# Memory values head by head in 256 columns, and the feed-forward's activation sums moved: at once in layer 0, over four products in layer 1

## The chip, the core and the metric

The kernel runs on one NeuronCore of a Trainium2 chip. Its engines are TensorE (PE: matmuls, and PEld: its weight loads), VectorE (DVE), ScalarE (ACT), GpSimd (POOL, which here only issues DMAs that accumulate) and SyncE (SP, which issues the other DMAs). The metric is the device time of one execution in microseconds, as a median of several runs.

## The reference, cut to what matters

Two decoder layers over x (512 tokens of 1024), with 256 memory tokens:

```python
z = rmsnorm(h, g_mix[i]) @ w_in[i]
# layer 0: causal pooling over 2, 4, 8, 16 tokens; layer 1: differential attention, 4 heads
mem_out = memory_attention(z_memq, mem, g_mem[i], w_mem_kv[i])    # 4 heads of 256
h = h + jnp.concatenate([mix, mem_out], axis=-1) @ w_out[i]
h = h + swiglu(rmsnorm(h, g_ffn[i]), w_gate[i], w_up[i], w_down[i])    # 2816 hidden
```

All is float32. The memory's values are the second half of `rmsnorm(mem) @ w_mem_kv[i]`: 256 tokens by 4 heads of 256 columns.

## The kernel before, in words

**Numbers as two halves.** Every float32 operand is split into a rounded part `hi` (an ACT copy, line 174 or 177) and the rest `lo` (a DVE subtraction, line 175 or 178); a product is three matmuls, hi·hi, hi·lo and lo·hi (`three`). So each 512 KB weight tile costs one ACT and one DVE instruction of 1024 columns ahead of its 12 or 24 matmuls. `weights()` loads and splits two tiles ahead (`AHEAD`); there are three buffers each for the raw tile and its halves (`N_W`).

**The order.** PE's instructions stay in the order in which the code is written; `Pace` writes it by interleaving generators on a rough clock, in which "rest" and "need" hold a task back. The other engines' orders come from the tile framework's scheduler; each engine then runs its queue in order. `FIRST` (layer 0) and `SECOND` (layer 1) list the units of the stage ahead of the output projection: `q`, `k`, `v` are the queries, keys and values of memory heads, `i` and `o` the pooling's input and output products, `Q`, `K`, `V` those of the differential attention, `h`, `a`, `b` tiles of the output projection. A star makes a unit wait until the previous head's scores are done. Beside it runs `mem_chain`: for each head scores (`msc`), softmax, transposes (`mtr`), split (`mpth`, `mptl`), and the product with the values (`mo`).

**Memory values.** `mem_values(l, b)` makes two heads at once: stationary the memory tokens, moving 512 columns of weights, 48 matmuls in four weight tiles, and two PSUM banks. `token_major`, used for the differential values `V`, makes one head from two weight tiles with 256 moving columns.

**Feed-forward.** `ffn_up` works on blocks of 512 hidden columns and replaces eight quarter products by seven (numbered 1 to 7, run in the order 1, 2, 5, 3, 6, 7, 4; 24 matmuls each). Products 5, 6, 3, 7 need sums of activations: `Norm7.__call__` splits `h[k]` as each output tile of the projection is finished, and in the first block (u = 0) `later` makes the sums: `sums124` during product 1 (for q = 0 to 3: `xs`, `xt`, `xc`, `xe`) and `sum3` during product 2 (`xd`, `xa`). Products 1 and 6, 7, 4 use PSUM tiles `ffr`, product 2 `ffz`, products 5 and 3 `ffq`. After product 5 its result is copied out (`c`, line 721) before product 3 goes on in the same bank. The SiLU (line 738) waits for the norm's factor `rcf`, which a chain of small DVE instructions makes from transposed sums of squares (`ps_st`, lines 281 to 316).

Of the kernel before, what the change touches and what calls it, by code (L numbers as in the profile page):

```python
# [8 lines left out]
F32 = mybir.dt.float32  # L9
# [3 lines left out]
AF = mybir.ActivationFunctionType  # L13
ALU = mybir.AluOpType
AX = mybir.AxisListType

P = 128
D = 1024
S = 512
NM = 256  # L20
DFF = 2816
KD = D // P
# [9 lines left out]
G_MIX, G_FFN, G_MEM, G_KV, G_FINAL, G_POOL, G_SUB = 0, 16, 32, 48, 56, 64, 72  # L32
# [4 lines left out]
AHEAD = 2  # L37
AHEAD7 = 2
EARLY7 = 2
R_H = 3.3  # L40
R_SM = 6.6
R_T = 1.98
R_DP = 4.4
# [11 lines left out]
R_N1 = 1.0  # L55
OUT = ((0, 1), (2, 3), (4, 5), (6,), (7,))
R_C = 4.5
SECOND = "Q0 k0 q0 k1 v0 q1* Q1 k2 q2* Q2 k3 v1 Q3 q3* K0 h0 h1 h2 V0 h3 h4 K1 V1 h5 K2 V2 K3 a0 a1 a2 V3 a3 h6 h7 b0 b2 b1 b3"
WARM = (256, 256, 256, 256)
FIRST = "q0 q1 k0 i0 i2 i1 o0 k1* v0 o1 i3 o2 k2 v1 q2* o3 k3 q3*"  # L60
PARTS = 2
START = "x0 p0 x1 x2 x3 p1 x4 x5 s0 r0 x6 x7 s1 w3 r1 s2 s3 r2 r3 s4 s5 s6 s7"

# [39 lines left out]
def trunk(ctx, tc, xT, memT, w_in, w_out, w_out1, w_gate, w_up, w_down, w_mk, w_mv, pool_w, w_k, w_v,  # L103
          gains, lams, c_ident, c_mask, c_rope, c_cnt, out):
    nc = tc.nc
# [14 lines left out]
    def slot(name, shape=(2, S), dtype=F32R, parts=P):  # L120

        return slots.tile([parts, *shape], dtype, tag="s", name=name)
# [7 lines left out]
    def duo(name):  # L130

        t = slot(name)
        return t[:, 0, :], t[:, 1, :]

    def tt(name="t"):
        return tmp.tile([P, S], F32, tag="t", name=name)

    def mmps(name="mm"):
        return ps_mm.tile([P, S], F32, tag="mm", name=name)
# [31 lines left out]
    def split(src, hi, lo, scale=None):  # L171

        if scale is None:
            queued(A.copy(out=hi, in_=src))  # L174
            queued(V.tensor_tensor(out=lo, in0=src, in1=f(hi), op=ALU.subtract))  # L175
        else:
            queued(A.activation(out=hi, in_=src, func=AF.Copy, scale=scale))
            queued(V.scalar_tensor_tensor(out=lo, in0=src, scalar=scale, in1=f(hi), op0=ALU.mult, op1=ALU.subtract))


    class Load:
# [4 lines left out]
        def __init__(self, src, kt, cols):  # L186
            self.src, self.kt, self.cols = src, kt, cols
# [4 lines left out]

        def part(self, ks):
            raw, hi, lo = [t[:, ks, :] for t in (self.raw, self.hi, self.lo)]
            if len(self.src.shape) == 3:
                nc.sync.dma_start(out=raw, in_=self.src[:, ks, :])
            else:

                raw, hi, lo = raw.rearrange("p n (k c) -> p n k c", k=2), *[t.rearrange("p k (n c) -> p n k c", n=2) for t in (hi, lo)]
                nc.sync.dma_start(out=raw, in_=self.src)  # L200
            split(raw, hi, lo)

        def fetch(self):
# [17 lines left out]
    def weights():  # L221

        used[0] += 1
        load_to(used[0] + (AHEAD if isinstance(plan[min(used[0], len(plan) - 1)], Load) else AHEAD7))
        return loaded[used[0] - 1]

    def unit(loads, go, need=None):
        plan.extend(x if hasattr(x, "parts") else Load(*x) for x in loads)
        return go, need
# [11 lines left out]
    def gain(base, k):  # L241
        return g_sb[:, base + k:base + k + 1]
# [87 lines left out]
    class Norm7:  # L330
# [1 line left out]

        def __init__(self, base, minus):
            self.base, self.minus, self.sums = base, minus, Sums()
            self.of, self.xa = {n: [None] * 4 for n in (1, 2, 3, 4, 5, 6, 7)}, [None] * 4

        def __call__(self, k):
            q, of = k % 4, self.of  # L340
            if k < 4:
                a, b = self.xa[q] = duo("xa")
                split(h[k][:, :NM], a[:, :NM], b[:, :NM], gain(self.base, k))
                of[1][q] = a[:, :NM], b[:, :NM]
            else:
                a, b = duo("xb")
                split(h[k], a, b, gain(self.base, k))
                of[2][q], of[4][q] = (a[:, :NM], b[:, :NM]), (a[:, NM:], b[:, NM:])
            self.sums.add(h[k])

        def sums124(self, q):
            g, gq, mq = gain(self.base, q + 4), gain(self.base, q), self.minus[:, q:q + 1]
            one, two = slice(0, NM), slice(NM, S)
            x, t = tt("xs"), tt("xt")
            A.activation(out=x, in_=h[q + 4], func=AF.Copy, scale=g)
            V.scalar_tensor_tensor(out=t[:, one], in0=h[q][:, two], scalar=gq, in1=x[:, two], op0=ALU.mult, op1=ALU.subtract)
            V.scalar_tensor_tensor(out=t[:, two], in0=h[q][:, one], scalar=mq, in1=t[:, one], op0=ALU.mult, op1=ALU.add)
            a, b = duo("xc")
            split(t, a, b)
            self.of[5][q], self.of[6][q] = (a[:, one], b[:, one]), (a[:, two], b[:, two])  # L360
            V.tensor_tensor(out=x[:, one], in0=x[:, one], in1=t[:, two], op=ALU.add)
            if q % 2 == 0:
                self.last = duo("xe")
            a, b = [x_[:, (q % 2) * NM:(q % 2 + 1) * NM] for x_ in self.last]
            split(x[:, one], a, b)
            self.of[3][q] = a, b

        def sum3(self, q):
# [5 lines left out]

        def later(self, product, i):

            for q in (2 * i, 2 * i + 1):
                if product == 1:
                    self.sums124(q)
                elif product == 2:  # L380
                    self.sum3(q)

    def x_split(base, k, xs):
        a, b = duo("x")
# [86 lines left out]

        return unit([(src[c], 4, 256) for c in range(2)], go)

    def mem_values(l, b):


        def go():
            pss = [mmps("v") for _ in range(2)]
            x = mem_x[l]
            for i in range(KD // 2):  # L480
                whi, wlo = weights()
                for k in range(2):
                    xh, xl = x[0][2 * i + k], x[1][2 * i + k]
                    for t, ps in enumerate(pss):
                        tk = slice(t * P, (t + 1) * P)
                        yield from group(ps, three(xh[:, tk], xl[:, tk], whi[:, k, :], wlo[:, k, :]),
                                         i == 0 and k == 0, i == KD // 2 - 1 and k == 1)
            yield "spawn", leave(pss)

        def leave(pss):  # L490
            yield "need", "m_row"
            heads = [duo("v") for _ in range(2)]
            for t, ps in enumerate(pss):
                for n, (a, b_) in enumerate(heads):
                    i, o = slice(n * 256, (n + 1) * 256), slice(t * 256, (t + 1) * 256)
                    split(ps[:, i], a[:, o], b_[:, o], m_col[:, t:t + 1])
            for n, v in enumerate(heads):
                mem_v[l, 2 * b + n] = [v]
                pace.at(("mv", l, 2 * b + n), 5.0)

        return unit([(w_mv[l, 2 * b:2 * b + 2, i // 2, :, 2 * (i % 2):2 * (i % 2) + 2, :].rearrange("n p k c -> p n k c"), 2, 2 * 256)
                     for i in range(KD // 2)], go)


    def mem_queries(l, n, xs, need=None, at_once=False):
# [167 lines left out]
    def ffn_up(l, norm, rc, hid):  # L673
        def one(u):
# [6 lines left out]
            def product(p, pss, start=False):  # L681
                more = {} if start else {"skip_group_check": True}

                def part(i, t, whi, wlo):
                    tk = slice(t * P, (t + 1) * P)
                    terms = []
                    for k in range(2):
                        xh, xl = norm.of[p][2 * i + k]
                        terms += [(xh[:, tk], whi[:, k, :]), (xl[:, tk], whi[:, k, :]), (xh[:, tk], wlo[:, k, :])]
                    yield from group(pss[t][:, :w], terms, start and i == 0, i == 1, **more)  # L690

                if p in (5, 7):

                    ws = [weights() for _ in range(2)]
                    for t in range(2):
                        for i in range(2):
                            yield from part(i, t, *ws[i])
                    return
                for i in range(2):
                    ws = weights()  # L700
                    if u == 0:
                        norm.later(p, i)
                    for t in range(2):
                        yield from part(i, t, *ws)
# [286 lines left out]
    norm0, norm1, xk = Norm(G_MIX), Norm(G_MIX + 8), ([], [])  # L991
    minus = const.tile([P, 2 * KD], F32, name="minus")
    V.tensor_scalar_mul(minus, g_sb[:, G_FFN:G_FFN + 2 * KD], -1.0)
    norm_f = [Norm7(G_FFN, minus[:, :KD]), Norm7(G_FFN + 8, minus[:, KD:])]
    rcf = [const.tile([P, NT], F32, name=f"rcf{l}") for l in range(2)]
    hid = [], []
    hids = [([], []), ([], [])]
# [259 lines left out]
```

## Time and profile before

| | us |
|---|---|
| median of 3 runs | 1378.43 (1378.07 to 1380.15) |
| the profiled execution, its own time | 1381.14 |
| its span, first to last instruction | 1379.4 |
| PE busy in the span | 1344.4 (97%) |
| DVE busy | 839.9 (61%) |
| ACT busy | 666.7 (48%) |

The span is cut below into stretches in which one can count the matmuls that have to run, at the rate that undisturbed stretches show; what a stretch takes beyond that is lost. PE's busy time alone doesn't show the loss, since a matmul at a lower clock is also busy.

### The profile page before, as it was taken

To read this page: it belongs to the slowest core of one execution; us is meant where nothing else is said; L and a number is where in the kernel's file an instruction comes from. 1 tells how busy PE (TensorE), PEld (TensorE's weight loads), DVE (VectorE), ACT (ScalarE), POOL (GpSimd) and SP (SyncE) were. 2 spreads that over 40 slices of the span, in tenths; PEclk is the share of its full clock that TensorE was granted. 3 is DMA by queue.
4 is the path that set the end of the run, shared out by engine and by line. 5 is a ranking of instruction groups with operands and counts; after the bars stand their busy time and mean duration, and the time that the engine had idled before them with its cause. 6 is when DMAs were issued, how large, how long until landed. Compare 5 with 4: busy or idle time off the path is not lost.

```text
span 1379.4 us, 17573 instructions
## 1 busy us (share of the span) xinstructions
PE 1344.4 (97%) x6746; PEld 1132.1 (82%) x6746; DVE 839.9 (61%) x1366; ACT 666.7 (48%) x1093; POOL 103.2 (7%) x84
## 2 busy tenths in 40 slices
PE   9998999989999999999999899999999999999997
PEld 7887888868888888888888788888877888888886
DVE  8877543575566584336556655678596655576323
ACT  7444432455555573324545534455375555556421
POOL 0000000022222200000000000000012222200000
PEclk9999999989999999999999999999999999999999
DMA  6343323588889913334423222221269899843331
GB/s 233 108 138 84 123 77 92 135 157 164 186 183 166 200 41 98 101 98 147 136 84 120 87 61 77 77 77 62 86 146 186 171 205 160 160 108 96 100 96 61
DMA packets 111156, 168.57 MB, mean 122 GB/s; under 512 B 5920, under 2 KB 84512, under 8 KB 111072
## 3 DMA queue, kind: packets, MB, share of 16 engines
q1 hardware_dynamic: 67856, 124.67, 28.7%
q0 software_dynamic: 42240, 41.95, 20.0%
q8 instruction: 53, 0.87, 0.3%
q10 hardware_dynamic: 976, 0.82, 0.2%
q14 instruction: 31, 0.25, 0.1%
HBM read 165.33 MB, written 2.10 MB: 121 GB/s over the span
## 4 chain that ended last, share of the span: by engine, by line
PE 71%; DVE 4%; ACT 2%; issue 1%; DMA 1%; POOL 0%; DVEq 0%; ACTq 0%; POOLq 0%
PE down L151 17%; PE ffr L151 16%; PE qk L151 6%; PE ffq L151 6%; PE wo L151 6%; PE v L151 5%; PE ffz L151 4%; PE mq L151 3%; PE mk L151 2%; PE htr L154 1%; DVE wlo L175 1%; PE dsc L151 1%; PE do L151 1%; ACT whi L174 1%; PE msc L151 1%; PE mo L151 1%
## 5 line engine op out<-in xcount | busy, mean ns | idle before, releaser
L175 DVE TENSOR_TENSOR wlo<-raw,whi 128x1024 fp32r<-128x1024 f32 (+2 forms) x226 | 267.7, 1186 | 257.1 <-ACT whi L174 256.5
L174 ACT CAST whi<-raw 128x1024 fp32r<-128x1024 f32 (+2 forms) x226 | 230.9, 1022 | 392.5 <-PE down L151 120.3
L151 PE MATMUL down<-hidp,whi 128*128 128x512 f32 (+1 forms) x748 | 220.4, 378 | 1.8 <-ACT hidp L174 1.1
L175 DVE TENSOR_TENSOR wlo<-rawa,whi 128x1024 fp32r<-128x1024 f32 (+1 forms) x108 | 117.3, 1086 | 85.5 <-ACT whi L174 81.8
L151 PEld LDWEIGHTS down<-hidp,whi 128*128 128x128 f32 x748 | 137.5, 188 | 28.3 <-ACT hidp L174 1.6
L174 ACT CAST whi<-rawa 128x1024 fp32r<-128x1024 f32 (+1 forms) x108 | 101.6, 941 | 104.9 <-PE ffr L151 58.7
L151 PE MATMUL down<-hidp,wlo 128*128 128x512 f32 (+1 forms) x374 | 140.9, 377 | 0.0
L646 POOL DMA_DIRECT2D rawa<-in_w_up x40 | 51.5, 1287 | 1038.7 <-DVE wlo L175 1007.4
L151 PE MATMUL ffr<-whi,xa 128*128 128x512 f32 (+1 forms) x384 | 112.1, 376 | 0.0
L151 PEld LDWEIGHTS down<-hidp,wlo 128*128 128x128 f32 x374 | 70.4, 188 | 12.9
L151 PE MATMUL mq<-x,whi 128*128 128x512 f32 x256 | 80.0, 393 | 0.8 <-ACT whi L174 0.6
L151 PE MATMUL qk<-x,whi 128*128 128x512 f32 x256 | 80.7, 397 | 0.0
L151 PE MATMUL wo<-mo,whi 128*128 128x512 f32 x256 | 79.4, 392 | 0.0
L151 PEld LDWEIGHTS ffr<-whi,xa 128*128 128x128 f32 x384 | 68.7, 189 | 11.8 <-ACT c L726 0.4
L151 PE MATMUL ffr<-wlo,xa 128*128 128x512 f32 (+1 forms) x192 | 71.5, 372 | 0.0
L151 PE MATMUL ffq<-whi,xe 128*128 128x512 f32 (+1 forms) x192 | 57.8, 385 | 3.7 <-ACT c L721 3.1
L151 PEld LDWEIGHTS mq<-x,whi 128*128 128x128 f32 x256 | 47.8, 189 | 11.7 <-ACT whi L174 1.6
L151 PE MATMUL ffq<-whi,xc 128*128 128x512 f32 (+1 forms) x192 | 57.2, 383 | 0.0
L151 PE MATMUL ffr<-whi,xb 128*128 128x512 f32 (+1 forms) x192 | 55.7, 374 | 0.4 <-DVE c L731 0.4
L151 PE MATMUL ffz<-whi,xb 128*128 128x512 f32 (+1 forms) x192 | 55.6, 373 | 0.0
L151 PEld LDWEIGHTS qk<-x,whi 128*128 128x128 f32 x256 | 47.8, 190 | 9.4
L151 PEld LDWEIGHTS wo<-mo,whi 128*128 128x128 f32 x256 | 47.4, 188 | 9.4
(234 smaller groups left out, 2712.2 us busy)
## 6 DMA issues: line engine op xcount, KB each, us to landing
rawa<-in_w_up POOLq DMA_DIRECT2D x40, 512.0 KB, 6.0
raw<-in_w_down SPq DMA_DIRECT2D x34, 512.0 KB, 3.6
raw<-in_w_out SPq DMA_DIRECT2D x32, 512.0 KB, 3.5
raw<-in_w_in SPq DMA_DIRECT2D x30, 512.0 KB, 3.8
raw<-in_w_gate SPq DMA_DIRECT2D x20, 512.0 KB, 4.8
rawa<-in_w_gate SPq DMA_DIRECT2D x20, 512.0 KB, 5.8
raw<-in_w_up SPq DMA_DIRECT2D x20, 512.0 KB, 5.0
raw<-in_w_up POOLq DMA_DIRECT2D x20, 512.0 KB, 6.1
```

The source lines that it names most:

```text
L151: tc.keep_in_program_order(nc.tensor.matmul(ps, lhsT=l, rhs=r, start=start, stop=stop, **more))
L154: tc.keep_in_program_order(nc.tensor.transpose(out=out, in_=in_, identity=ident))
L174: queued(A.copy(out=hi, in_=src))
L175: queued(V.tensor_tensor(out=lo, in0=src, in1=f(hi), op=ALU.subtract))
L646: nc.gpsimd.dma_start(out=t, in_=src, accum_op=ALU.add)
```

## The change

Five edits.

1. `mem_values` becomes a call of `token_major` for one head: 48 matmuls with 256 moving columns and two weight tiles a head. The special form in `Load.part` goes.
2. `FIRST` and `SECOND` list the four heads' values apart and in other places. In layer 0: v0, then `o1`, v1, then `i3`; v2 before `q3`, v3 last. In layer 1: v0, then `q1`, v1; v2 and v3 between `q3` and `K0`.
3. `sums124` is cut into `sum1`, `sum2`, `sum4`; `xc` is split in two halves of 256 columns, and its source `xt` lies in a slot for two q's. In layer 0 (`at_once`) all four sums of a q are made when `h[q + 4]` is finished, within the output projection.
4. In layer 1 they are made in the first block during four products: `sum1` in 1, `sum4` in 2, `sum2` in 5, `sum3` in 3.
5. `R_H`, the rest ahead of the hidden transposes, is 3.7 instead of 3.3.

```diff
-R_H = 3.3
+R_H = 3.7
...
-SECOND = "Q0 k0 q0 k1 v0 q1* Q1 k2 q2* Q2 k3 v1 Q3 q3* K0 h0 h1 h2 V0 h3 h4 K1 V1 h5 K2 V2 K3 a0 a1 a2 V3 a3 h6 h7 b0 b2 b1 b3"
+SECOND = "Q0 k0 q0 k1 v0 q1* v1 Q1 k2 q2* Q2 k3 Q3 q3* v2 v3 K0 h0 h1 h2 V0 h3 h4 K1 V1 h5 K2 V2 K3 a0 a1 a2 V3 a3 h6 h7 b0 b2 b1 b3"
-FIRST = "q0 q1 k0 i0 i2 i1 o0 k1* v0 o1 i3 o2 k2 v1 q2* o3 k3 q3*"
+FIRST = "q0 q1 k0 i0 i2 i1 o0 k1* v0 o1 v1 i3 o2 k2 q2* o3 k3 v2 q3* v3"
...
+            if self.at_once and k >= 4:
+                for part in (self.sum1, self.sum2, self.sum4, self.sum3):
+                    part(q)
+
+        def sum1(self, q):
+
+            x, one, two = tt("xs")[:, :NM], slice(0, NM), slice(NM, S)
+            A.activation(out=x, in_=h[q + 4][:, two], func=AF.Copy, scale=gain(self.base, q + 4))
+            if q % 2 == 0:
+                self.pair = slot("xt", (2, S), F32)
+            t = self.raw[q] = self.pair[:, q % 2, :]
+            V.scalar_tensor_tensor(out=t[:, one], in0=h[q][:, two], scalar=gain(self.base, q), in1=x, op0=ALU.mult, op1=ALU.subtract)
+            V.scalar_tensor_tensor(out=t[:, two], in0=h[q][:, one], scalar=self.minus[:, q:q + 1], in1=t[:, one],
+                                   op0=ALU.mult, op1=ALU.add)
+            a, b = self.xc[q] = duo("xc")
+            split(t[:, one], a[:, one], b[:, one])
+            self.of[5][q] = a[:, one], b[:, one]
+
+        def sum2(self, q):
+            a, b = [x_[:, NM:] for x_ in self.xc[q]]
+            split(self.raw[q][:, NM:], a, b)
+            self.of[6][q] = a, b
+
+        def sum4(self, q):
+            x = tt("xs")[:, :NM]
+            V.scalar_tensor_tensor(out=x, in0=h[q + 4][:, :NM], scalar=gain(self.base, q + 4), in1=self.raw[q][:, NM:],
+                                   op0=ALU.mult, op1=ALU.add)
...
         def later(self, product, i):
 
-            for q in (2 * i, 2 * i + 1):
-                if product == 1:
-                    self.sums124(q)
-                elif product == 2:
-                    self.sum3(q)
+            if not self.at_once:
+                for q in (2 * i, 2 * i + 1):
+                    {1: self.sum1, 2: self.sum4, 5: self.sum2, 3: self.sum3}.get(product, lambda q: None)(q)
...
+    def mem_values(l, n):
+        return token_major(w_mv[l, n], lambda: mem_x[l], 2, m_col, mem_v, ("mv", l, n), "m_row")
...
                     ws = [weights() for _ in range(2)]
+                    if u == 0:
+                        norm.later(p, 0)
+                        norm.later(p, 1)
...
-    norm_f = [Norm7(G_FFN, minus[:, :KD]), Norm7(G_FFN + 8, minus[:, KD:])]
+    norm_f = [Norm7(G_FFN, minus[:, :KD], True), Norm7(G_FFN + 8, minus[:, KD:], False)]
```

Where instructions move. PE, layer 1, scores of memory head 3 (`msc`), ahead of `K0` (`qk`). Before:

```order
L151 MATMUL mq<-x,wlo 128x512
L151 MATMUL msc<-mk,mq 128x256 x24
L154 MATMUL mtr<-ident,mp 128x128 x4
L151 MATMUL qk<-x,whi 128x512 x2
L151 MATMUL qk<-x,wlo 128x512
L151 MATMUL qk<-x,whi 128x512 x2
L151 MATMUL qk<-x,wlo 128x512
L154 MATMUL mtr<-ident,mp 128x128 x4
```

Now (`v` are the values of head 3, `mo` is head 2):

```order
L151 MATMUL mo<-mptl,v 128x512
L151 MATMUL mo<-mpth,v 128x512
L151 MATMUL msc<-mk,mq 128x256 x24
L151 MATMUL v<-whi,m 128x256
L151 MATMUL v<-wlo,m 128x256
L151 MATMUL v<-whi,m 128x256 x2
L151 MATMUL v<-wlo,m 128x256
```

The scores no longer stand right behind the last query matmuls but 12 value and output products later, and 12 `qk` matmuls and the other half of `v` follow before the first transpose.

DVE, layer 0, around the split of head 1's probabilities (`mptl`). Before, with the window sums of pooling group 3 (`u`, `win`, `pooled`) and the eviction of `py` (`mix`):

```order
L822 TENSOR_TENSOR win<-win 128x510
L175 TENSOR_TENSOR wlo<-raw,whi 128x1024
L822 TENSOR_TENSOR win<-win 128x508
L175 TENSOR_TENSOR mptl<-mtr,mpth 128x2x256
L822 TENSOR_TENSOR win<-win 128x504
L175 TENSOR_TENSOR wlo<-raw,whi 128x2x2x256
L826 SCALAR_TENSOR_TENSOR pooled<-win,u 128x496
L828 TENSOR_TENSOR pooled<-win,cnt 128x16
L829 TENSOR_TENSOR pooled<-pooled,u 128x16
L175 TENSOR_TENSOR p<-pooled,p 128x512
L178 SCALAR_TENSOR_TENSOR mix<-py,g_sb,mix 128x512 x2
```

Now:

```order
L175 TENSOR_TENSOR wlo<-raw,whi 128x512
L178 SCALAR_TENSOR_TENSOR v<-v,m_col 128x256
L175 TENSOR_TENSOR mptl<-mtr,mpth 128x2x256 x2
L803 TENSOR_TENSOR u<-z,rb_121 128x512
L807 TENSOR_TENSOR win<-u 128x511
L175 TENSOR_TENSOR wlo<-raw,whi 128x1024
L807 TENSOR_TENSOR win<-win 128x510
L807 TENSOR_TENSOR win<-win 128x508
L175 TENSOR_TENSOR mo<-mo 128x512
L807 TENSOR_TENSOR win<-win 128x504
L175 TENSOR_TENSOR mo<-mo 128x512
```

The split of the probabilities stands ahead of the window sums instead of among them, and the eviction `mix` is no longer behind them and ahead of this head's `mo`.

DVE, layer 0, from the last sums up to the first weights of product 5 (`wlo<-rawa`). Before:

```order
L175 TENSOR_TENSOR xc<-xt,xc 128x512
L361 TENSOR_TENSOR xs<-xs,xt 128x256
L357 SCALAR_TENSOR_TENSOR xt<-h_92,minus,xt 128x256
L356 SCALAR_TENSOR_TENSOR xt<-h_93,g_sb,xs 128x256
L175 TENSOR_TENSOR xe<-xs,xe 128x256
L361 TENSOR_TENSOR xs<-xs,xt 128x256
L175 TENSOR_TENSOR xc<-xt,xc 128x512
L357 SCALAR_TENSOR_TENSOR xt<-h_93,minus,xt 128x256
L175 TENSOR_TENSOR xe<-xs,xe 128x256
L361 TENSOR_TENSOR xs<-xs,xt 128x256
L281 TENSOR_REDUCE var<-ps_st 128x4
L175 TENSOR_TENSOR wlo<-rawa,whi 128x1024
```

Now, from the first sum of q = 3 (the other three q's stand earlier, among the output projection's tiles):

```order
L357 SCALAR_TENSOR_TENSOR xt<-h_93,g_sb,xs 128x256
L175 TENSOR_TENSOR wlo<-raw,whi 128x1024
L358 SCALAR_TENSOR_TENSOR xt<-h_93,minus,xt 128x256
L175 TENSOR_TENSOR xc<-xt,xc 128x256
L371 SCALAR_TENSOR_TENSOR xs<-h_97,g_sb,xt 128x256
L381 TENSOR_TENSOR xd<-h_93 128x256
L276 TENSOR_REDUCE var<-ps_st 128x4
L175 TENSOR_TENSOR xc<-xt,xc 128x256
L175 TENSOR_TENSOR xe<-xs,xe 128x256
L178 SCALAR_TENSOR_TENSOR xa<-xd,g_sb,xa 128x256
L278 TENSOR_SCALAR var<-var 128x4
L175 TENSOR_TENSOR wlo<-rawa,whi 128x1024
```

Ahead of the weights stand the sums of one q instead of four, with `xd` and `xa` of that q among them.

## Rows read from the trace of the kernel before

**Rows 1.** The page: busy time and share of the span, by engine.

```profile
PE 1344.4 (97%) x6746; PEld 1132.1 (82%) x6746; DVE 839.9 (61%) x1366; ACT 666.7 (48%) x1093; POOL 103.2 (7%) x84
```

**Rows 2.** Waits of PE: waiter, releaser: total us, times, longest.

```profile
PE ffq L151 <- DVE wlo L175: 6.6, 4, 1.9
PE mo L151 <- DVE mix L178: 3.2, 1, 3.2
PE ffq L151 <- ACT c L721: 3.1, 3, 2.7
...
PE mtr L154 <- DVE mp L554: 2.5, 1, 2.5
```

**Rows 3.** Stretches: from:to, length, busy by engine, PEclk, DMA, GB/s.

```profile
116.75:129.61 12.86, 8.94 (x50) 7.49 (x49) 8.12 (x13) 4.09 (x7) 0.00 (x0) 0.87 0.30 83
780.72:796.99 16.27, 11.85 (x51) 9.82 (x50) 10.54 (x21) 9.38 (x19) 0.00 (x0) 0.79 0.14 43
276.74:328.05 51.31, 45.56 (x188) 36.00 (x187) 35.12 (x63) 30.34 (x48) 10.32 (x8) 0.90 0.78 163
328.05:368.69 40.64, 40.39 (x185) 33.03 (x185) 23.84 (x24) 22.75 (x33) 10.29 (x8) 1.00 0.91 180
1021.24:1067.78 46.54, 41.78 (x190) 33.34 (x189) 35.77 (x64) 30.22 (x48) 10.34 (x8) 1.00 0.85 178
249.00:271.00 22.00, 22.00 (x99) 18.23 (x98) 12.20 (x16) 8.40 (x13) 2.71 (x2) 1.00 0.50 123
```

**Rows 4.** The chain of waits, pieces: start us, us, what.

```profile
313.78 1.06 PE htr L154 x8
...
640.30 5.75 PE mk L151 x48
...
659.83 2.88 PE msc L151 x24
...
682.90 2.72 PE mo L151 x12
...
745.50 10.91 PE v L151 x48
```

**Rows 5.** Timeline of PE, both memory stages: start, us, what, [idle before].

```profile
122.48 0.80 PE L151 MATMUL mo<-mpth,v 128*128 128x512 f32 x1 [3.24 <-DVE mix L178]
...
783.65 4.00 PE L151 MATMUL msc<-mk,mq 128*128 128x256 f32 x19 [0.88 <-DVE mq L175]
...
790.16 0.81 PE L154 MATMUL mtr<-ident,mp 128*128 128x128 f32 x4 [2.50 <-DVE mp L554]
```

**Rows 6.** Timeline of DVE and PE, start of the layer 0 feed-forward.

```profile
271.14 0.69 DVE L590 TENSOR_TENSOR h<-wo,h 128x512 f32<-128x512 f32 x1 [2.31 <-PE wo L151]
...
276.38 0.48 DVE L356 SCALAR_TENSOR_TENSOR xt<-h,g_sb,xs 128x256 f32<-128x256 f32 x1
276.78 0.42 DVE L361 TENSOR_TENSOR xs<-xs,xt 128x256 f32<-128x256 f32 x1
...
283.51 1.22 DVE L175 TENSOR_TENSOR wlo<-rawa,whi 128x1024 fp32r<-128x1024 f32 x1
...
284.79 0.50 PE L151 MATMUL ffq<-wlo,xc 128*128 128x512 f32 x1 [1.89 <-DVE wlo L175]
...
294.93 1.28 ACT L738 ACT_TABLE_LOAD   x1
...
298.08 0.74 PE L151 MATMUL ffq<-whi,xe 128*128 128x512 f32 x2 [2.69 <-ACT c L721]
```

**Rows 7.** Timeline of DVE and PE, start of the layer 1 feed-forward.

```profile
1031.00 0.50 PE L151 MATMUL ffq<-wlo,xc 128*128 128x512 f32 x1 [1.86 <-DVE wlo L175]
...
1036.14 1.22 DVE L175 TENSOR_TENSOR wlo<-raw,whi 128x1024 fp32r<-128x1024 f32 x1
...
1037.41 0.50 PE L151 MATMUL ffq<-wlo,xe 128*128 128x512 f32 x1 [1.88 <-DVE wlo L175]
```

**Rows 8.** Groups by form: count | busy us, mean ns | idle before.

```profile
L151 PEld LDWEIGHTS v<-whi,x 128*128 128x128 f32 x256 | 40.7, 191 | 0.1
```

More of the change, by code (lines that the diff above doesn't have):

```diff
@@ L194, in part @@
             raw, hi, lo = [t[:, ks, :] for t in (self.raw, self.hi, self.lo)]
[L195 to L200, printed above, removed]
+            nc.sync.dma_start(out=raw, in_=self.src[:, ks, :])
             split(raw, hi, lo)
@@ L330, in trunk, with __init__ @@
     class Norm7:
-        def __init__(self, base, minus):
-            self.base, self.minus, self.sums = base, minus, Sums()
+        def __init__(self, base, minus, at_once):
+            self.base, self.minus, self.at_once, self.sums = base, minus, at_once, Sums()
+            self.raw, self.xc = {}, {}
             self.of, self.xa = {n: [None] * 4 for n in (1, 2, 3, 4, 5, 6, 7)}, [None] * 4
@@ L349, in __call__ @@
             self.sums.add(h[k])
[L351 to L361, printed above, removed]
+            if self.at_once and k >= 4:
[21 more added lines that the diff above has]
+                                   op0=ALU.mult, op1=ALU.add)
             if q % 2 == 0:
@@ L364, in sums124 @@
             a, b = [x_[:, (q % 2) * NM:(q % 2 + 1) * NM] for x_ in self.last]
-            split(x[:, one], a, b)
+            split(x, a, b)
             self.of[3][q] = a, b
@@ L472, in token_major @@
         return unit([(src[c], 4, 256) for c in range(2)], go)
[L474 to L502, printed above, removed]
+    def mem_values(l, n):
+        return token_major(w_mv[l, n], lambda: mem_x[l], 2, m_col, mem_v, ("mv", l, n), "m_row")
     def mem_queries(l, n, xs, need=None, at_once=False):
```

## The prediction, made before the run

> **What bounds the kernel now.** I read the busy shares first: PE is busy for 1344.4 of 1379.4 us, 97%, no other engine for more than 61% [rows 1]. So the kernel is bound by PE, and a change gains in two ways only: fewer or cheaper matmuls, or less idle or slowly clocked PE. The table of PE's waits comes second, because it says where PE idles and on whom [rows 2]: four waits for the low half of feed-forward weights (6.6 us), waits for the copy `c` of a product's bank (3.1), one for the eviction `mix` (3.2), one for the probabilities `mp` (2.5). Third come stretches around those waits [rows 3], because an idle PE is followed by a lower granted clock and the waits alone are too small a measure. The reader is to see there that the clock is 1.00 in a steady block of the feed-forward and 0.79 to 0.90 in three of the four places.
>
> For each place I count what has to run. At full clock 48 matmuls of 512 columns take 10.91 us, 0.2273 each; 48 of 256 take 5.75, 0.1198 each; 24 scores take 2.88; 12 products with the values 2.72; 8 transposes 1.06 [rows 4].
>
> - Memory, layer 0, 116.75 to 129.61: 12 `mo` and 36 `mk` need 2.72 + 36 x 0.1198 = 7.03; the stretch takes 12.86. Lost: 5.83.
> - Memory, layer 1, 780.72 to 796.99: 24 `msc`, 18 `qk`, 8 transposes need 2.88 + 18 x 0.2273 + 1.06 = 8.03 of 16.27. Lost: 8.2.
> - First feed-forward block, layer 0: 51.31 against 40.64 for the block behind it. Lost: 10.67.
> - First block, layer 1: 46.54 against 40.64. Lost: 5.90, at full clock, so here it is waits.
>
> All four, 30.6 us, are what this change can give. The rest of the program keeps its order on PE.
>
> **The price: narrower values.** Per pair of heads 48 matmuls of 512 columns become 96 of 256. Over two layers 192 x 0.2273 = 43.64 becomes 384 x 0.1198 = 46.00: **+2.36 us**, on PE, so on the path. The 16 weight tiles, their DMAs on SP's queue, the splits and the evictions keep their number and size; one PSUM bank less is held at a time. Three weight buffers are now held by one head's values rather than by two heads'; the tightest place is the start of the third head's values in layer 1, where the program order leaves the load about 0.6 us of slack. I cost it at nothing, covered by the 48 matmuls of the head ahead (5.75 us), and if that cover fails, at one ACT and DVE handoff of about 1 us, as the smallest of the four weight waits (6.6 - 1.89 - 1.88 - 1.86 = 1.0 [rows 2, 6, 7]); it lies inside the bounds.
>
> The rate of 0.1198 us rests on `mk`, whose stationary side is as wide. Every weight load lasts 191 ns by its own row [rows 8], longer than the matmul it precedes, so it must lie beside other matmuls in those 5.75 us. The Trainium skill, page "TensorE: Matmul & The Clock Gate", Part 3, "The mechanism", says that a load overlaps with matmuls in flight only when its row group differs, which it doesn't here. By that page the loads would be serial; with the page's load figure of about 107 ns for 128 columns ("LDWEIGHTS") an estimate is 0.21 us a matmul and +36 us for the change instead of +2.36. The trace's 48 in 5.75 us disagrees, and the sum goes by the trace.
>
> **Memory, layer 0.** `mo` waits 3.24 us for `mix` [rows 5], because its second bank is freed by an eviction that stands on DVE behind the window sums of a pooling group. In the new order the split `mptl` comes ahead of those sums and `mix` is no longer between. What waits behind `mptl` now is the window sums, whose result `py` needs later, with other products ahead of it. The smaller wait for the split, 0.7 us, I leave in place: gain 5.83 - 0.7 = **5.1**. Bounds: 2 (the sums or a bank still delay `mo` by half, and the clock stays low) to 5.83.
>
> **Memory, layer 1.** Scores stand right behind the last queries, wait 0.88 us for their split, then the first transpose waits 2.50 for the softmax [rows 5], and the clock is 0.79 [rows 3]. Now 12 value products and 12 `mo` (1.44 + 2.72 = 4.2 us) stand ahead of the scores, and 24 value products and 12 `qk` (2.88 + 2.73 = 5.6 us) between scores and transpose. Each cover is over twice the wait. I leave one wait of about 1 us, for `mo` of head 2 now needs values that were finished only just ahead: gain 8.2 - 1.0 = **7.2**. Bounds: 3 (covers fail by half; the clock stays down) to 8.2.
>
> **Feed-forward, layer 0.** After the last `h` tile (271.14) DVE does 18 sums and splits of the activations, beside other work, before the first weights of product 5, whose low half begins at 283.51 and is finished for PE at 284.79, 1.89 after PE asked (282.90) [rows 6]. In the new order only one q's sums remain there: two weight splits (1.22), `xb`, `acc`, `var` (0.7 each), nine small ones (0.4 to 0.5), then the weights: about 10 us by the durations in those rows instead of 12.4, so the weights come at about 281.8, plus some handoffs to ACT within. That is just ahead of 282.90. The second pair follows 1.2 to 2.5 us later, at 283.0 to 284.3, against 284.3 asked (six matmuls of 0.2273 after the first). The work moved goes into the output projection: per q four instructions of 0.48 and four of 0.42, 3.60 us for each of three pairs of `h` tiles. In that stretch DVE is busy 12.20 of 22.00 us [rows 3], or 6.04 per pair of `h` tiles (10.9 us of PE); 6.04 + 3.60 = 9.64, 88% full. That cover holds on the mean, with little to spare.
>
> The third wait, 2.69 us for the copy `c`, comes from ACT: a table load and two SiLUs stand ahead of it from 294.93 [rows 6]. They wait for `rcf`, whose small instructions now stand between the weights. PE will ask earlier, at 282.90 + 30 x 0.2273 = 289.7 (30 matmuls stand between). From the table load to PE's going on took 298.08 - 294.93 = 3.15. I put `rcf` 2.6 to 4.0 behind the second weights of 284.3 (five to eight of its instructions of 0.5), so at 286.9 to 288.3, and PE goes on at 290.0 to 291.4: a wait of 0.3 to 1.7 stays. I take 1.2, nearer the upper end, because handoffs between engines aren't in it. Before, 5.6 us of waits cost 10.67, a factor of 1.9, the rest being low clock; 1.2 x 1.9 = 2.3. Gain 10.67 - 2.3 = **8.4**. Bounds: 5 (the copy waits as now, 2.69 x 1.9) to 10.67.
>
> **Feed-forward, layer 1.** Here the sums stay behind the `h` tiles, but `sum3` (per q a 0.42 and a 0.48), and half of each `xc` split (0.27 per q, 0.69 against 0.42) go behind product 5's and 3's weights: 3.6 + 1.1 less 0.24 of added starts, 4.4 us less ahead of them. The weights of product 5 that came at 1031.00 have four half splits less ahead of them, and come at about 1029.8; PE asks at 1029.14 (1031.00 - 1.86). Product 3's, finished at 1037.36, have all 4.4 us less ahead of them, so 1032.9, or up to 1.8 later where the moved sums are made in between; PE asks at 1037.41 - 1.88 - 1.86 = 1033.67 [rows 7]. So 0.7 and, in the middle of that stretch, 0.1 of the 3.74 us stay. The other 2.1 us of the 5.90 lie elsewhere in the block, and no edit touches them. Gain 5.90 - 2.9 = **3.0**. Bounds: 0 (the sums delay the next weights as much) to 4.8 (both waits gone and half of the rest).
>
> `R_H` moves no instruction of PE, and the branch taken out of the load was never on a wait: nothing.
>
> **Sum.** 2.36 - 5.1 - 7.2 - 8.4 - 3.0 = **-21.3**. Against the profiled execution, 1381.14: 1359.8. Its time is 2.7 above the median 1378.43 of the runs, so **1357.1** as a median. Most: 2.36 - 29.5 = -27.1, 1351.3. Least: 2.36 - 10 = -7.6, 1370.8.
>
> **The rivals.**
>
> *DVE stays the bound at both feed-forward starts.* For it: 88% on the mean of the output projection says nothing of its order, and late `h` tiles push `rcf` and the product weights alike. Against it: the last `h` add waited 2.31 us for PE, so DVE has slack there [rows 6]. With the lower bounds 5 and 0: 2.36 - 5.1 - 7.2 - 5 - 0 = -14.9, **1363.5**.
>
> *The memory waits only move.* The waits that go are for splits in DVE's queue, and the next head's split may stand behind other work. Against it: the covers above. With 2 and 3: 2.36 - 2 - 3 - 8.4 - 3 = -14.0, **1364.4**. Both rivals together: **1370.8**.
>
> *Weight loads bound the narrow matmuls, and it is slower.* Place: the 384 value products, where the stationary side (memory tokens) changes at every matmul while the moving side is now as short as the load. Price: at one load of 191 ns per matmul [rows 8], 384 x 0.191 = 73.3 against 43.64, +29.7; with the gains of the forecast, 23.7, that is +6.0, **1384.4**. It decides from (43.64 + 23.7) / 384 = 0.175 us a matmul. Against it: `mk`, 0.1198 with the same loads. The Trainium skill's rule in "The mechanism" of "TensorE: Matmul & The Clock Gate", above, would have it so.
>
> *The change doesn't do what it says:* the new covers are there in the order, but each place finds another last wait, and gains and price cancel within 0.2%.
>
> **How the numbers follow.** Forecast 0.66; DVE rival 0.11; memory rival 0.12; both 0.04; loads 0.05; cancelled 0.02. Range 1351 to 1369: the forecast's own bounds and the first two rivals, leaving out the last three cases (0.11) and the rim of the forecast. A change under 0.2% (2.8 us) can't be told from none by measuring; by the cases, faster 0.93, same 0.02, slower 0.05.
>
> **What would show it.** Right: values at 0.12 us a matmul, 5.75 per head; granted clock near 1.00 in both memory stages; no `mo` wait for `mix`, no `mtr` wait for `mp` over 1 us; the first feed-forward block about 43 us in layer 0 and 43.5 in layer 1; DVE near 88% busy late in layer 0's output projection; one wait for `c` of 1 to 2 us left. Wrong: values at 0.19 us; a new wait of `mo` for values or of PE for a `wo` weight in the output projection; a clock below 0.9 in the four places though the waits are short.

## The result, and the profile after

| | before | after |
|---|---|---|
| median of the runs, us | 1378.35 | 1356.95 (1355.3 to 1358.52) |
| the profiled execution, us | 1381.14 | 1358.52 |
| its span, us | 1379.4 | 1356.7 |

The ratio is 0.9842, interval 0.9825 to 0.9859: faster by 1.6%, 21.4 us.

The page of the kernel after, busy time by engine, answers to [rows 1]:

```profile
PE 1337.0 (99%) x6938; PEld 1137.0 (84%) x6938; DVE 841.0 (62%) x1374; ACT 665.3 (49%) x1101; POOL 103.1 (8%) x84
```

PE has 192 matmuls more and is busy for 7.4 us less. A matmul at a lower clock counts as busy for longer, so less busy time for more matmuls means less time at a low clock; the idle time has shrunk too, from 35.0 us to 19.7 (span less busy time). The waits of PE (waiter, releaser: total us, times, longest) answer to [rows 2]:

```profile
PE ffq L151 <- ACT c L706: 3.1, 4, 2.0
...
PE ffq L151 <- DVE wlo L175: 0.2, 1, 0.2
```

The weight waits have gone from 6.6 us to 0.2, those for `mix` and `mp` don't appear, and neither do the scores'. What is left of the four places are waits for the copy `c`: 0.67 us in layer 0, where it was 2.69 before, and a new one of 2.00 us in layer 1.

Stretches of the kernel after (length, busy by engine PE, PEld, DVE, ACT, POOL, then the granted clock, DMA share and GB/s) answer to [rows 3]: both memory stages, then both first feed-forward blocks.

```profile
100.00:124.17 24.17, 24.17 (x139) 21.17 (x138) 19.22 (x30) 12.22 (x24) 0.00 (x0) 1.00 0.30 98
765.09:781.33 16.24, 16.24 (x99) 14.42 (x98) 12.74 (x24) 10.17 (x20) 0.00 (x0) 1.00 0.25 81
271.86:313.24 41.38, 40.47 (x188) 33.12 (x187) 27.54 (x43) 25.00 (x38) 10.26 (x8) 1.00 0.94 195
1000.15:1044.99 44.84, 42.60 (x190) 34.56 (x188) 35.80 (x66) 29.50 (x50) 10.31 (x8) 0.96 0.89 184
```

In both memory stages PE is busy for the whole stretch at clock 1.00. In the layer 1 stage 99 matmuls and transposes fit into 16.24 us, where before 51 took 16.27; 24 of the 99 are value products of 256 columns. In the last 22.00 us of layer 0's output projection DVE is busy for 17.95 us, 82% where the prediction had 88%, and PE waits for no `wo` weight. The first block of layer 0 is 0.74 above a steady block (40.64), that of layer 1 still 4.2.

To put the time in its places, this table cuts each profiled execution at the first matmul of product 2 (`ffz`) in the first and the second block of each layer, read from the timeline of PE; e1 to e11 are the experiments below. Each number is the length of a piece in us.

| kernel | start to block 1 of layer 0 | block 1, layer 0 | on to block 1 of layer 1 | block 1, layer 1 |
|---|---|---|---|---|
| before | 276.74 | 51.14 | 693.36 | 46.38 |
| after | 271.86 | 41.38 | 686.91 | 44.84 |
| e1 narrow values, old places | 271.89 | 51.09 | 693.76 | 46.21 |
| e2 narrow values, new places | 271.68 | 50.45 | 686.32 | 46.60 |
| e3 sums at once, layer 0 alone | 277.26 | 41.34 | 693.38 | 46.86 |
| e4 sums spread, layer 1 alone | 278.04 | 51.18 | 693.68 | 44.35 |
| e5 after, at once in both | 272.08 | 41.30 | 686.93 | 47.02 |
| e7 after, copy `c` first | 272.80 | 41.30 | 686.34 | 41.80 |
| e8 after, spread in both | 271.45 | 44.03 | 686.41 | 42.18 |
| e9 as e5, copy `c` first | 271.64 | 41.30 | 686.36 | 46.88 |
| e10 after, one head behind | 271.82 | 41.56 | 688.25 | 44.72 |
| e11 after, no head behind | 271.90 | 41.83 | 694.15 | 44.81 |

Before to after: -4.9, -9.8, -6.4, -1.5, and nothing behind, together 22.6 us; the rounded spans differ by 22.7. The same code varies by 1.3 us in the first piece (276.7 to 278.0 in before, e3 and e4).

### The profile page after: what moved, and what is told of

Read it like the earlier page. It is cut to its first block, busy times and chain, and to the rows that moved or that the text cites. A ratio compares the mean times of both kernels' runs of the same rounds, so it can differ in the third digit from the quotient of the medians.

```text
span 1356.7 us, 17958 instructions
## 1 busy us (share of the span) xinstructions
PE 1337.0 (99%) x6938; PEld 1137.0 (84%) x6938; DVE 841.0 (62%) x1374; ACT 665.3 (49%) x1101; POOL 103.1 (8%) x84
## 4 chain that ended last, share of the span: by engine, by line
PE 92%; DVE 3%; ACT 2%; DMA 1%; issue 1%; SPq 0%; DVEq 0%; ACTq 0%; POOLq 0%
PE down L151 17%; PE ffr L151 17%; PE wo L151 12%; PE v L151 7%; PE ffq L151 7%; PE mq L151 6%; PE qk L151 6%; PE ffz L151 4%; PE mk L151 3%; PE z L151 3%; PE msc L151 2%; PE mo L151 2%; PE htr L154 1%; DVE wlo L175 1%; PE dsc L151 1%; PE do L151 1%
## 5 line engine op out<-in xcount | busy, mean ns | idle before, releaser
L151 PEld LDWEIGHTS ffr<-whi,xa 128*128 128x128 f32 x384 | 68.8, 189 | 11.4
L151 PEld LDWEIGHTS mq<-x,whi 128*128 128x128 f32 x256 | 47.7, 188 | 11.6 <-ACT whi L174 1.7
L151 PE MATMUL ffr<-whi,xc 128*128 128x512 f32 (+1 forms) x192 | 55.1, 371 | 0.0
```

The source lines that it names most:

```text
L151: tc.keep_in_program_order(nc.tensor.matmul(ps, lhsT=l, rhs=r, start=start, stop=stop, **more))
```

## The experiments

**The values alone, and their places.** e1 is the kernel before with narrow values only.

```diff
-SECOND = "... k1 v0 q1* ... k3 v1 Q3 q3* K0 ..."
+SECOND = "... k1 v0 v1 q1* ... k3 v2 v3 Q3 q3* K0 ..."
-FIRST = "... v0 o1 i3 o2 k2 v1 q2* ..."
+FIRST = "... v0 v1 o1 i3 o2 k2 v2 v3 q2* ..."
-    def mem_values(l, b):
+    def mem_values(l, n):
+        return token_major(w_mv[l, n], lambda: mem_x[l], 2, m_col, mem_v, ("mv", l, n), "m_row")
```

> The kernel before with the memory values made head by head in 256 columns and nothing else: two heads' values stand one behind the other where the pair stood, sums and rest are the old ones. Theory: only the price shows, 384 x 0.1198 - 192 x 0.2273 = +2.4 us, so 1380.8 us, each head's 48 products take 5.75 us, and the waits of PE for the eviction mix (3.2), the probabilities mp (2.5) and the scores' operands (0.9 and 1.0) stay, because they belong to the order. Rival, the loads bound the narrow products: 48 x 0.191 = 9.2 us a head, 1408 us. Second rival, the finer unit and not the order ended the waits: 1372 us or less, and mix and mp are gone from the waits.

Measured: 1376.07 us, ratio 0.9969 (0.9955 to 0.9983), 2.3 us faster where +2.4 was expected. The waits of PE in e1:

```profile
PE mtr L154 <- DVE mp L556: 3.1, 1, 3.1
...
PE msc L151 <- ACT mq L174: 1.0, 1, 1.0
...
PE msc L151 <- DVE mq L175: 0.9, 1, 0.9
```

Layer 1's waits stay, as the theory says, and its stretch is 0.4 us longer (table). But layer 0's wait for `mix` is gone, and all of layer 0's 4.9 us come from the narrowing. The summaries of `mo` between 88 and 124 us show that it comes earlier: before (first line) and e1 (second), with count, durations in ns, first and last start.

```profile
L151 PE MATMUL mo<-mpth,v x15: 388/389/796, 97.9 to 123.9; 128*128 128x512 f32 x15
```

```profile
L151 PE MATMUL mo<-mpth,v x16: 389/389/396, 89.8 to 111.3; 128*128 128x512 f32 x16
```

With a pair, the first head's `mo` has to wait for both heads' values; alone, v0 is done after 48 short products, so `mo`, the scores of head 1 and its `mo` all come earlier, the last one (108.84 to 111.7) ahead of pooling group 3's `py` (from 115.64) rather than behind it. On DVE (timeline of e1) the eviction `mix` of the group before is done by then, and the split `mptl` stands ahead of the window sums of group 3:

```profile
102.03 1.40 DVE L178 SCALAR_TENSOR_TENSOR mix<-py,g_sb,mix 128x512 fp32r<-128x512 f32 x2
...
106.89 0.69 DVE L175 TENSOR_TENSOR mptl<-mtr,mpth 128x512 fp32r<-128x512 f32 x1 [1.13 <-ACT mpth L174]
107.66 0.69 DVE L823 TENSOR_TENSOR u<-z,rb 128x512 f32<-128x512 f32 x1
```

This is the order on DVE that the prediction read in the kernel after; the narrowing alone brings it. The second rival was right for layer 0 and wrong for layer 1. The rival of the loads falls: of the kernel after, the chain of waits has a head's 48 values in one piece (start, us, what),

```profile
95.52 5.76 PE v L151 x48
```

and by form the loads beside them last as long as ever (count | busy us, mean ns | idle before):

```profile
L151 PEld LDWEIGHTS v<-whi,m 128*128 128x128 f32 x256 | 40.8, 192 | 0.1
```

0.120 us per product with a load of 192 ns each: the loads lie beside other matmuls.

e2 is e1 with the new `FIRST` and `SECOND` of the change, the sums as before.

> The narrow values and their new places in both lists; the activation sums as in the kernel before. Theory: the waits for mix, mp and the scores' operands go, and the first feed-forward blocks stay as they were (51.1 and 46.4 us). From the two traces the stretch up to the layer 0 feed-forward is 4.9 us shorter and the one between the two first blocks 6.5, so -11.3: 1367.1 us. By the prediction's own terms 2.36 - 5.1 - 7.2 = -9.9: 1368.4. Rival, part of these gains came from the moved sums (which leave DVE emptier or fuller around the stages): above 1371.

Measured: 1367.45 us, ratio 0.9907 (0.9888 to 0.9927). The theory holds: the first blocks take 50.5 and 46.6 us, layer 0 gains 0.2 more than in e1, layer 1 gains 7.4 more. So the new `SECOND` is worth all of its layer, and the new `FIRST` nothing that can be told from none.

**Where in layer 1.** e11 and e10 change one thing in the kernel after: how many heads' values stand behind the last queries.

```diff
-SECOND = "... k3 Q3 q3* v2 v3 K0 ..."
+SECOND = "... k3 v2 v3 Q3 q3* K0 ..."    (e11)
+SECOND = "... k3 v2 Q3 q3* v3 K0 ..."    (e10)
```

> The changed kernel with no values behind the last queries of layer 1: heads 2 and 3 ahead of the last `Q`, so scores stand right behind the queries and the transposes right behind the scores, as before; head 1's values stay in the new place. Theory: the whole layer 1 gain of the order lies in this one place. The waits for the scores' operands (1.0 and 0.9) and for mp (2.5 to 3.1) come back with a low clock, the stretch between the two first blocks is 693.8 us as with narrow values in the old places, +6.9 against the changed kernel: 1363.9 us. Rival, the place of head 1's values or the emptier DVE took part in it: 1360 or less.

Measured: 1365.62 us, ratio 0.9909 (0.9887 to 0.9931), and the stretch is 694.15 us, 7.2 more than in the kernel after. PE's waits there, timeline of e11 (start, us, what, idle before and its releaser):

```profile
769.79 0.50 PE L151 MATMUL msc<-mk,mq 128*128 128x256 f32 x2 [1.04 <-ACT mq L174]
771.17 2.54 PE L151 MATMUL msc<-mk,mq 128*128 128x256 f32 x19 [0.88 <-DVE mq L175]
776.80 0.81 PE L154 MATMUL mtr<-ident,mp 128*128 128x128 f32 x4 [3.10 <-DVE mp L536]
```

They are the waits of [rows 5] again, with 3.10 us for the transposes where it was 2.50. One place, behind the last queries, holds the whole layer 1 gain of the order; head 1's new place has no part that shows.

What stands in that place in the kernel after, by the chain of waits (start, us, what):

```profile
753.88 8.63 PE v L151 x72
762.51 2.75 PE mo L151 x12
765.26 2.87 PE msc L151 x24
768.13 2.88 PE v L151 x24
771.01 2.75 PE qk L151 x12
```

Ahead of the scores stand all 48 value products of head 2 and 24 of head 3, then 12 `mo`: 11.4 us, and not the 12 values and 12 `mo`, 4.2 us, of the prediction (the description of the change has 12 products in all). The second cover, 5.6 us, is as they have it.

> The changed kernel with only head 3's values behind the last queries of layer 1, and head 2's ahead of the last `Q`: ahead of the scores now stand 24 value products (2.9 us), between scores and first transpose the other 24 (2.9 us) and no `qk`. Theory, cover is what counts and the softmax needs 2.5 us of it: no wait over 0.5 us, the stretch between the two first blocks within 1 us of the changed kernel's 686.9, 1357 us. Rival, the prediction's wide covers (4.2 and 5.6 us) were needed, with the second transpose right behind the first now late: 2 us or more longer, with a wait for mp.

Measured: 1358.88 us, ratio 0.9858 (0.9839 to 0.9878); the stretch is 1.3 us longer than after, which lies between the two expectations. Of e10, timeline of PE:

```profile
772.29 0.81 PE L154 MATMUL mtr<-ident,mp 128*128 128x128 f32 x4 [1.33 <-DVE mp L536]
```

24 values (2.9 us) cover the scores' operands wholly, but the transposes only in part: the first four go on time, the second four wait 1.33 us. So 2.9 of the 11.4 us ahead of the scores are enough, and for the second transposes more than 2.9 us are needed; in the kernel after they have 5.6 us and six `qk` besides. How much is needed between the two no run shows.

**Layer 0's sums alone.** e3 is the kernel before with the new sums, at once in layer 0, and the old `sums124` in layer 1.

```diff
-    norm_f = [Norm7(G_FFN, minus[:, :KD]), Norm7(G_FFN + 8, minus[:, KD:])]
+    norm_f = [Norm7(G_FFN, minus[:, :KD], "once"), Norm7(G_FFN + 8, minus[:, KD:], "old")]
```

> The kernel before with the sums of layer 0 made at once within the output projection, and nothing else; values wide and in their old places, layer 1 with the old sums. Theory: the first block of layer 0 falls from 51.1 to 41.4 us as in the trace after, the output projection is not longer, 1368.6 us. Prediction's term: -8.4, 1370.0. Rival, DVE stays the bound (its lower bound 5): 1373.4, with waits of PE in the output projection for weights of wo. Memory waits stay as before.

Measured: 1372.73 us, ratio 0.9947 (0.9931 to 0.9962). The ratio's interval stands for 5.2 to 9.5 us less. The block is 41.34 us, 9.8 less, and the output projection is not longer, as the theory says; yet the medians (1378.38 and 1372.73) differ by 5.7 only. Against the profiled execution of before, e3's is 8.8 us faster (1381.14 to 1372.30). That execution of before lay 2.7 above its median, while e3's lay at the low end of its runs. Where the other executions of before were faster, no trace shows; this stays open. So the lengths in the table hold for the traced executions, and by medians the three parts (e2 -10.9, e3 -5.7, e4 -3.0) come to -19.6 of the -21.4 us.

**Layer 1's sums alone.** e4 has the old sums in layer 0 and the spread ones in layer 1 (`"old"`, `"spread"` in the line above), the rest as before.

> The kernel before with the sums of layer 1 spread over products 1, 2, 5 and 3, and nothing else. Theory: the weight waits (1.86 and 1.88 us) fall to 0.2 or less, but the copy c is now queued on ACT behind a weight cast that waits for an accumulating DMA, and PE waits 2.0 us for it, after which the clock is halved for a while: first block 44.8 us against 46.4, 1376.9 us. Prediction's term: -3.0, 1375.4. Rival, that late cast came only of the earlier arrival in the kernel after, so the block is 42 us: 1374.

Measured: 1375.38 us, ratio 0.9969 (0.9958 to 0.998), -3.0. The block is 44.35 us with one wait of 1.51 us for `c`, between theory and rival. But the traced execution, at 1380.91, lies 5.5 us above the median of its nine: its block is 2.0 shorter than before while its first piece is 1.3 longer, and its span (1379.1) is hardly shorter at all. So the trace shows the new wait, and not where the median's 3.0 lie.

**The new wait in layer 1.** Timeline of ACT in the kernel after, the two copies `c` and the casts between them:

```profile
1009.05 0.59 ACT L706 COPY c<-ffq 128x512 f32<-128x512 f32 x1
1010.18 1.06 ACT L174 CAST whi<-raw 128x1024 fp32r<-128x1024 f32 x1 [0.54 <-PE ffq L151]
1014.01 1.04 ACT L174 CAST whi<-rawa 128x1024 fp32r<-128x1024 f32 x1 [2.77 <-DMA rawa<-in_w_up]
1014.96 0.58 ACT L706 COPY c<-ffq 128x512 f32<-128x512 f32 x1
```

and of PE and POOL:

```profile
1015.59 0.88 PE L151 MATMUL ffq<-whi,xe 128*128 128x512 f32 x2 [2.00 <-ACT c L706]
```

```profile
1005.65 1.28 POOL L628 DMA_DIRECT2D rawa<-in_w_up  x1 [12.48 <-DVE xs L371]
```

The second copy needs only PE's bank, but on ACT it stands behind the cast of product 6's first weights. That cast waits for an accumulating DMA, issued at 1005.65 and used at 1014.01, 8.4 us later, and PE waits behind the copy. Then PE runs at its lower clock level, 1.2 GHz, until 1019.3 (a matmul of 512 columns each 0.43 us instead of 0.23), and the clock is 0.96 over the block. e7 puts the copy ahead of that cast and moves no other instruction.

```diff
-                    A.copy(out=c22[t], in_=q[t][:, :w])
+                    (tc.keep_in_program_order if (l, u) == (1, 0) else lambda x: x)(A.copy(out=c22[t], in_=q[t][:, :w]))
...
-            queued(A.copy(out=hi, in_=src))
+            (tc.keep_in_program_order if act_order else queued)(A.copy(out=hi, in_=src))
```

Here `act_order` is true for the one cast.

> The changed kernel with one ACT instruction moved: in the first feed-forward block of layer 1 the second copy c of product 5's bank stands ahead of the cast of product 6's first weights, which waits for an accumulating DMA (in the trace after it idles 2.77 us for it, and PE 2.00 us for the copy behind it). Theory: that order is what is left of layer 1's loss; the first block falls from 44.8 to about 41.5 us like that of layer 0, no wait of PE for c over 0.7, 1353.6 us. Rival, the DMA comes that late only in some executions, so the median gains half, 1355.3. Second rival, the late DMA moves the wait on to product 6's weights: same block, 1357.

Measured: 1355.62 us (1354.65 to 1356.59), ratio 0.9839 (0.9826 to 0.9852). ACT in e7:

```profile
1010.47 1.06 ACT L174 CAST whi<-raw 128x1024 fp32r<-128x1024 f32 x1 [0.54 <-PE ffq L151]
1012.01 0.59 ACT L706 COPY c<-ffq 128x512 f32<-128x512 f32 x1 [0.49 <-PE ffq L151]
1012.87 1.05 ACT L174 CAST whi<-rawa 128x1024 fp32r<-128x1024 f32 x1 [0.27 <-DMA rawa<-in_w_up]
```

The wait is gone and the block is 41.80 us, 3.0 less, as the theory says; the median is 1.3 lower, near the first rival's, though 0.5 of that the kernel before shows too (1377.87 beside e7, 1378.35 beside the kernel after). Both fit together if the DMA is late by differing amounts. From issue to the start of its cast it took 8.4 us in the kernel after, 8.3 in e11, 8.2 in e10, 7.9 in e4, 7.3 in e8 (1007.39 to 1014.68) and 6.9 in e7. With the copy behind the cast, PE's wait for it follows: 2.00, 1.96, 1.87, 1.51 and 0.95 us; in e8 the block took 42.18. The kernel after has executions at 1355.3 and 1355.7 and others at 1358.2 and 1358.5, and the one traced, with the 2.00 us, is of the latter; that the former have a shorter wait is inferred from e8 and not traced. Whether e7 is faster than the kernel after can't be told by the two intervals.

**At once or spread.** e8 spreads the sums in layer 0 too, e5 makes them at once in layer 1 too, e9 is e5 with the copy first.

```diff
-    norm_f = [Norm7(G_FFN, minus[:, :KD], True), Norm7(G_FFN + 8, minus[:, KD:], False)]
+    norm_f = [Norm7(G_FFN, minus[:, :KD], "spread"), Norm7(G_FFN + 8, minus[:, KD:], "spread")]    (e8)
+    norm_f = [Norm7(G_FFN, minus[:, :KD], "once"), Norm7(G_FFN + 8, minus[:, KD:], "once")]    (e5, e9)
```

> The changed kernel with the sums spread over products 1, 2, 5 and 3 in layer 0 as well. Theory: the first block of layer 0 gets what layer 1 has, 44.8 us with a wait for the copy c behind the cast that waits for the accumulating DMA, instead of 41.4: +3.4, 1360.3 us. Rival, spreading is as good and at-once is not needed: 1357, block under 42.5. Third, the order of ACT comes out otherwise and DVE's weight waits return: block 47 or more, 1363.

Measured: 1359.78 us, ratio 0.987 (0.9856 to 0.9883). Layer 0's block takes 44.03 us, with waits of 0.75 for weights and 2.15 for `c`, against 41.38 with the sums at once: the theory, with 2.7 of the 3.4 us.

> The changed kernel with the sums made at once in layer 1 as well. Theory: DVE has the room in layer 1's output projection too, the weight splits of product 5 and with them the accumulating DMAs come earlier, so the wait for c behind the cast falls under 1 us and the first block from 44.8 to 42.5 us: 1354.5 us. Rival, DVE is the bound there (3.6 us more per pair of tiles): PE waits in the output projection for weights or at the first product, block or projection longer by 2 us or more: 1359.

Measured: 1360.47 us, ratio 0.9873 (0.986 to 0.9887): the rival, by the time. The wait for `c` does go, but PE waits in product 2 (timeline of PE, e5):

```profile
1006.32 0.51 PE L151 MATMUL ffz<-whi,xb 128*128 128x512 f32 x1 [2.45 <-ACT xb L177]
1007.98 0.50 PE L151 MATMUL ffz<-whi,xb 128*128 128x512 f32 x1 [1.16 <-DVE xb L178]
```

Its operand `xb` of the last `h` tile is late on both engines that make it. The first wait ended with ACT's part, which stands behind a weight cast that waits for an accumulating DMA, and behind the casts of the sums (timeline of ACT, e5):

```profile
1003.58 1.04 ACT L174 CAST whi<-rawa 128x1024 fp32r<-128x1024 f32 x1 [1.36 <-DMA rawa<-in_w_up]
1004.53 0.40 ACT L174 CAST xc<-xt 128x256 fp32r<-128x256 f32 x1
1004.84 0.40 ACT L174 CAST xe<-xs 128x256 fp32r<-128x256 f32 x1
1005.15 0.50 ACT L177 ACTIVATE xa<-xd,g_sb 128x256 fp32r<-128x256 f32 x1
1005.56 0.71 ACT L177 ACTIVATE xb<-h,g_sb 128x512 fp32r<-128x512 f32 x1
```

The second ended with DVE's, behind the sums of the q ahead and a weight split (timeline of DVE, e5):

```profile
1004.97 0.43 DVE L175 TENSOR_TENSOR xc<-xt,xc 128x256 fp32r<-128x256 f32 x1 [0.59 <-ACT xc L174]
1005.31 0.42 DVE L175 TENSOR_TENSOR xe<-xs,xe 128x256 fp32r<-128x256 f32 x1
1005.64 1.22 DVE L175 TENSOR_TENSOR wlo<-rawa,whi 128x1024 fp32r<-128x1024 f32 x1
1006.78 0.48 DVE L178 SCALAR_TENSOR_TENSOR xa<-xd,g_sb,xa 128x256 fp32r<-128x256 f32 x1
1007.18 0.75 DVE L178 SCALAR_TENSOR_TENSOR xb<-h,g_sb,xb 128x512 fp32r<-128x512 f32 x1
```

Layer 1's DVE is fuller in the last 22.00 us of its projection: 16.97 us with the sums spread, 18.38 in e5, where layer 0 had 12.20 before the change and has 17.95 now. So the choice by layer fits the room that DVE has there, and the mechanism of the prediction's first rival is real in the layer where the change avoids it. It is not the whole cause: part of the first wait is the cast behind the DMA on ACT, and how much of the 2.45 us each gives no run separates.

> Sums at once in both layers, and the copy c ahead of the cast as in e7. Theory: both first blocks at 41.4 to 41.5 us, 1353.4 us, the same as with the sums spread and the copy first, because no wait of more than 0.7 us is left in either. Rival, at-once costs DVE time in layer 1's output projection: 2 us above the spread form.

Measured: 1360.77 us, ratio 0.9876 (0.9862 to 0.9889), like e5; block 46.88 us. The theory falls with e5's. The order of the copy has nothing to give where `xb` is late.

## Why the prediction was right, step by step

1357.1 us was forecast and 1356.95 measured. Against the profiled execution the sum was -21.3 and the spans differ by 22.7. By places the sizes differ, and they partly cancel.

- **Narrow values, +2.36.** Held: 5.76 us per head instead of 5.75. The Trainium skill's rule on loads ("TensorE: Matmul & The Clock Gate", Part 3, "The mechanism") would have cost +36 by the estimate given there; e1 and the rows above disagree with it for this shape. (From the 0.21 us given there the sum is 384 x 0.21 - 43.64 = 37.0. The same section also lets a load run ahead into a background weight buffer, so serial loads follow from its rule alone and not from the whole section.) The slower rival falls with it.
- **Memory, layer 0, -5.1 + 1.2 = -3.9.** Measured -4.9 in the whole stretch, where the same code varies by 1.3. The waits that were to go went, the 0.7 left for the split too. The order read on DVE was the right one, but its cause was mis-assigned: I read it off an order that holds both edits at once and counted it, in the expectation for e1 too, as the gain of the new places. e1 shows that the narrowing alone brings that order, through `mo`, which no longer waits for a second head's values.
- **Memory, layer 1, -7.2 + 1.2 = -6.0.** Measured -6.4; e11 confirms the place and the waits, and e10 that the transposes needed more than 2.9 us of cover. The cover ahead of the scores was misread, 4.2 us for 11.4, which did no harm since 2.9 are enough. The 1 us left for a late value didn't come: between head 2's last value and its `mo` stand 24 products of head 3, 2.9 us.
- **First block, layer 0, -8.4.** Measured -9.8. The weights of product 5 were placed 5.1 us behind the first `ffz` (281.8 - 276.74), against 6.2 when PE asks. The kernel after, DVE's timeline:

```profile
274.31 1.22 DVE L175 TENSOR_TENSOR wlo<-rawa,whi 128x1024 fp32r<-128x1024 f32 x1
...
275.94 1.23 DVE L175 TENSOR_TENSOR wlo<-rawa,whi 128x1024 fp32r<-128x1024 f32 x1
...
280.43 0.38 DVE L311 COPY rcf<-rc 128x4 f32<-128x4 f32 x1
```

They end 3.7 and 5.3 us behind it (271.86), so the waits go with room. The wait for `c` behind the table load and the SiLUs was foreseen at 0.3 to 1.7, taken as 1.2, and is there:

```profile
280.93 1.28 ACT L723 ACT_TABLE_LOAD   x1
282.22 1.34 ACT L723 ACTIVATE c<-c,rcf 128x512 f32<-128x512 f32 x2
283.47 1.03 ACT L174 CAST whi<-raw 128x1024 fp32r<-128x1024 f32 x1
284.40 0.57 ACT L706 COPY c<-ffq 128x512 f32<-128x512 f32 x1
```

```profile
285.03 0.73 PE L151 MATMUL ffq<-whi,xe 128*128 128x512 f32 x2 [0.67 <-ACT c L706]
```

The term was too small because the wait was 0.67 and not 1.2, and cost 0.74 and not 1.9 times itself: the clock stayed at 1.00. (In layer 1, 2.24 us of waits put the block 4.20 above a steady one, 1.9 times themselves, with the clock at 0.96.) That the wait came out within its range is in part luck, for its two pieces were both off: `rcf` was ready at 280.81, 9.0 us behind the first `ffz` where 10.2 to 11.6 were put, and from the table load to PE's going on it took 4.10 us and not 3.15, because a weight cast stands on ACT between the SiLUs and the copy. The prediction also read before as the table load and the SiLUs waiting for `rcf`, which was wrong. There `rcf` was ready at 292.73, and the table load at 294.93 came behind a cast that had waited for PE:

```profile
292.57 0.16 DVE L316 COPY rcf<-rc 128x4 f32<-128x4 f32 x1
```

```profile
293.86 1.05 ACT L174 CAST whi<-rawa 128x1024 fp32r<-128x1024 f32 x1 [0.74 <-PE ffq L151]
```

- **First block, layer 1, -3.0.** Measured -1.5 in the trace. The weight waits fell further than forecast (0.24 left), and the wait of 1.02 us of the hidden transposes, counted as untouched, is gone too, in e7 with the clock at 1.00 as well. The step that failed: only DVE's queue was followed, not ACT's, where the late cast stands ahead of the copy. Its 2.00 us and the low clock behind took 3.0 back (e7), in executions where the DMA is late.
- **`R_H`, nothing.** With 3.3 in place of 3.7 the kernel after becomes the same program, byte for byte, so there was nothing to run.

The first rival came true only in e5, and there in part; a wait that moved, as the second has it, shows only in e10, with the shorter cover. That the total fits to 0.2 us is partly luck, with terms off by 1.0, 0.4, 1.4 and -1.5 and medians that lie 1.6 and 2.7 below the profiled executions.

## What to carry to other kernels

Count what has to run in a stretch at undisturbed rates and take the difference, not the waits alone; it sized these gains within 1.5 us each against the traced executions. When two edits stand in one order, build the order of each alone before naming the cause. For every operand that is to come in time, walk the queue of each engine that makes it, ACT as well as DVE: an instruction that waits for a DMA holds up all that stands behind it, whatever it needs itself.

## What the runs showed of the hardware

The same accumulating DMA of 512 KB, at the same place in six builds, took 6.9 to 8.4 us from issue to the start of the cast that uses it, and in each this cast waited for the DMA last. In the five of them with the copy behind that cast PE waited 0.95 to 2.00 us, the longer the later the DMA. The kernel after has times some 3 us apart; that this DMA parts them is likely and not shown.

The length of a wait alone did not decide the clock behind it. In e8 PE waited 0.75 and 2.15 us in the first block of layer 0, and the granted clock stayed at 1.00 over the block (44.03 us, 3.4 above a steady one). In e4, 0.25 and 1.51 us in the first block of layer 1 left 0.96 (44.35 us, 3.7 above).
